# Spreading norm factors with one broadcast multiply and a float32 product, with sums and spreads called between contraction steps

## The chip, the cores and the metric

The kernel runs on one core of a Trainium2 chip. The metric is the device time of one execution in microseconds (us), lower being better; the runs of the kernel before took 1409.04 to 1411.53 us, with a median of 1411.13. Engines are named as in the profile: PE is TensorE's products, PEld its loads of the stationary operand, DVE is VectorE, ACT is ScalarE, POOL is GpSimd and SP issues most transfers.

## What is computed

A model of two layers over 512 tokens of width 1024, in float32. Layer 0 is a forgetting attention of 16 heads, layer 1 a latent attention (queries from 768, keys and values from 256 latent values, 16 heads, a rotary part of 64), and each layer ends in a gated feed-forward block with a convolution of width 3. What matters here is the norm, which stands in front of each block, twice more inside the latent attention and once at the end:

```python
def rmsnorm(x, g):
    y = x * lax.rsqrt(jnp.mean(x * x, axis=-1, keepdims=True) + EPS)
    return y * g

ckv = rmsnorm(x, kv_in_g) @ w_dkv
latent = rmsnorm(ckv[..., :KV_LORA], kv_norm_g)
k_rope = apply_rope(ckv[..., KV_LORA:], cos, sin)
q = rmsnorm(h @ w_dq, q_norm_g) @ w_uq
u = rmsnorm(x, ffn_norm) @ w_in
```

## The kernel before

Activations lie transposed: a tile has 128 features on the partitions and the 512 tokens as columns. Every weight and activation is split into a high and a low float32r part, and one contraction step (`mm3`, L82 to L85) is three products of 128x128 by 128x512: high by high, high by low, low by high. A projection tile is 8 such steps (6 or 2 from the latents) into one PSUM bank of the pool "acc", which has 3 banks; attention scores, transposes and the norms use the pool "att" with 5. `load_w` (L87) fetches a weight tile through SP, casts the high part on ScalarE (L104) and subtracts the low part on VectorE or GpSimd (L105).

A norm's factor belongs to a token, so it is needed along the columns, the same on all partitions. It is made in these steps. `Squares.add` (L137 to L145) squares a feature tile and adds it to a running sum. `rstd_of` (L147) contracts the sum with a vector of ones on TensorE, in four products of 128 tokens each (L153), so that the sums come out with tokens on the partitions, 128x4; VectorE scales them (L156) and GpSimd takes the power -0.5 (L158). `bcast_ps` (L161) spreads them back: it splits the factors into a float32r high part (the cast L165) and a low part (L166), scales the identity by each of the four columns of each part (eight operations of 128x128, L171) and contracts both 128x512 results with a matrix of ones (two float32r products, L172). `bcast` (L175) copies the result from PSUM on ScalarE (L179).

The norm is never applied to the input of a product but to its result. `Rstd.after` (L276) is called after each of the first tiles of a block: after the first complete tile it calls the sums, after the second the spread, and then it runs the evacuations that had to wait. `ffn` and `down` use it; `down` (L630) is a projection of the latent attention's preparation: six query tiles, then the rotary key tile, then two key/value tiles. Between these, in program order, stand the sums of the query norm (after the rotary key tile) and its spread (after the first key/value tile). `latents` (L637) multiplies a tile by the spread factors (L640) and splits it (L188 on ScalarE, L189 on VectorE). The first rotary product, `mm_rope(0)`, takes all six query latents. `turn` (L665) evacuates a rotary product: four copies of 32 partitions on ScalarE, which exchange halves (`swapped`, L647), then a multiply by the cosine on VectorE (L669). The key/value norm adds two squares (L145) and calls its sums after `mm_rope(0)`, its spread after the first query product, `proj_q(0)`.

The last norm of the program works on two halves of 256 tokens, with the second half's chain at the very end.

The program is written in the order above, and a planner puts the instructions of each engine into a fixed order: it takes what it expects to be ready, the earliest in the program first. Semaphores are placed by it too, and each engine then runs its list in order.

Of the kernel before, what the change touches and what calls it, by code (L numbers as in the profile page):

```python
# [15 lines left out]
P = 128  # L16
# [29 lines left out]
def tile_kernel(ctx, tc, xT_d, gains_d, bf_d, const_d, conv_d, wv_d, wq_d, wk_d, wfo_d,  # L46
# [77 lines left out]
    ones_r = cp.tile([P, P], F32R, name="ones_r")  # L124
    v.memset(f(ones_r), 1.0)
# [35 lines left out]
    def bcast_ps(r, m=NT):  # L161

        two = T(sp, [P, 2, NT], F32R, "two", 2)
        rh, rl = two[:, 0, :m], f(two[:, 1, :m])
        v.tensor_copy(rh, r)  # L165
        v.tensor_tensor(out=rl, in0=r, in1=f(rh), op=ALU.subtract)  # L166
        pt = att()[:, :m * P]
        for j, part in enumerate((f(rh), rl)):
            d = T(cp, [P, 512], F32R, "r2", R2)[:, :m * P]
            for i in range(m):  # L170
                v.tensor_scalar(out=d[:, i * P:(i + 1) * P], in0=idf, scalar1=part[:, i:i + 1], scalar2=None, op0=ALU.mult)  # L171
            pe.matmul(pt, ones_r, d, start=(j == 0), stop=(j == 1))  # L172
        return pt
# [95 lines left out]
    class Rstd:  # L269


        def __init__(self, squares):
            self.squares, self.step, self.R, self.todo = squares, 0, None, []

        def after(self, evacuate):
            if self.R is None:  # L276
                self.todo.append(evacuate)
                if self.step == 0:
                    self.r = rstd_of([self.squares.sum], D)
                else:  # L280
                    self.R = bcast(self.r)
                    for e in self.todo:
                        e(self.R)
                self.step += 1
            else:
                evacuate(self.R)


    def ffn(layer, xs, squares, gbase):
        with tc.tile_pool(name=f"ffn{layer}", bufs=1, reuse_waits="tile") as fp:  # L290
# [21 lines left out]
            for j in range(KF):  # L312
                for b in range(2):
                    wh, wl = load_w(wfi_d[layer, j, b], [P, KD, P])
                    pt = acc()
                    for k in range(KD):
                        mm3(pt, (wh[:, k, :], wl[:, k, :]), parts(xs, k), k == 0, k == KD - 1)
                    rstd.after(lambda R, j=j, b=b, pt=pt: evacuate(j, b, pt, R))
# [303 lines left out]
    with tc.tile_pool(name="ml", bufs=1, reuse_waits="tile") as mp:  # L622
# [7 lines left out]
        def down(w_d, gbase, dst):  # L630
            wh, wl = load_w(w_d, [P, KD, P], gain=(KD, gains[:, gbase:gbase + KD]))
            pt = acc()
            for k in range(KD):
                mm3(pt, (wh[:, k, :], wl[:, k, :]), parts(xs, k), k == 0, k == KD - 1)
            rstd.after(lambda R: v.tensor_tensor(out=dst, in0=pt, in1=R, op=ALU.mult))
# [29 lines left out]
        def turn(pt):  # L665

            c, t_ = r2(), r2()
            swapped(t_, pt, MSCALE)
            v.scalar_tensor_tensor(out=c, in0=pt, scalar=MSCALE, in1=cosT, op0=ALU.mult, op1=ALU.mult)  # L669

            def end():
                v.tensor_tensor(out=t_, in0=t_, in1=sinT, op=ALU.mult)
                v.tensor_tensor(out=c, in0=c, in1=t_, op=ALU.add)
                return c

            return end
# [55 lines left out]
        for j in range(KQ):  # L732
            down(wdq_d[j], G_MLA, qc[:, j, :])
            if j:
                for i in ((0, 1) if j == 1 else (j,)):
                    squares.add(qc[:, i, :], a, v if j == KQ - 1 else g)
# [3 lines left out]
        down(wdkv_d[KL], G_KVIN, krt)  # L740
        r = rstd_of([squares.sum], QL)
        down(wdkv_d[0], G_KVIN, qc[:, KQ, :])
        Rq = bcast(r, T(mp, [P, S], F32, "e3", 2))
# [8 lines left out]
        squares = Squares()  # L752
        for k in range(KL):
            squares.add(qc[:, KQ + k, :], a, v)
# [4 lines left out]
        r = rstd_of([squares.sum], KVL)  # L759
# [147 lines left out]
```

## Time and profile before

| what | value |
|---|---|
| median of 3 runs | 1411.13 us (1409.04 to 1411.53) |
| the profiled execution, its own time | 1410.6 us |
| its span, first to last instruction | 1408.8 us |
| TensorE busy | 1373.6 us, 98% of the span, 6594 products |
| VectorE, ScalarE, GpSimd busy | 886.6, 648.7 and 282.2 us |
| mean granted TensorE clock | 0.993 |

Busy time of TensorE is pipelined time: one entry's duration is longer than the distance to the next. Where a price is worked out, the distance between two starts is taken. An entry of a timeline shows in brackets how long its engine had been idle and what ended that. In a timeline, neighbouring entries of the same kind are merged, with their number behind the x.

### The profile page before, as it was taken

Reading aid. Unit: us, or ns where it says so; the run is one execution under the profiler, and the core shown is the slowest. Engines: PE = TensorE matmul, PEld = TensorE weight load, DVE = VectorE, ACT = ScalarE, POOL = GpSimd, SP = SyncE. Lnnn points to the kernel's source line nnn. Section 1 sums busy time; section 2 is a strip of 40 time slices with the busy share of each in tenths; the row PEclk is TensorE's granted clock in tenths of the full one; section 3 lists DMA queues with packets and bytes.
Section 4 is the critical chain, followed back from the end, with each engine's and each line's share of the span. In section 5 each row is a group of like instructions: output and inputs, shape, how many; then the busy total and the mean of one; then the engine's idle time right before and its main releaser. Section 6 shows DMA issues by size and latency. Waiting matters only on the chain. (4 is left out here: it accounts for less than half of the span.)

```text
span 1408.8 us, 17333 instructions
## 1 busy us (share of the span) xinstructions
PE 1373.6 (98%) x6594; PEld 1150.8 (82%) x6594; DVE 886.6 (63%) x1482; ACT 648.7 (46%) x1131; POOL 282.2 (20%) x214
## 2 busy tenths in 40 slices
PE   8999999899999999999899999999999999999997
PEld 7988888788888888888688888888888888888886
DVE  6667785677777754445866665575557777774333
ACT  4588884254444432223556555653234444442111
POOL 4343323500000001145422222212210000000222
PEclk9999999999999999999999999999999999999999
DMA  5321112232323233332121111212222322323331
GB/s 180 103 77 54 56 54 68 78 105 90 103 92 99 96 94 96 97 117 83 41 68 50 55 60 51 72 60 90 91 97 96 95 100 95 100 92 92 97 99 70
DMA packets 41252, 120.23 MB, mean 85 GB/s; under 512 B 5552, under 2 KB 9952, under 8 KB 41168
## 3 DMA queue, kind: packets, MB, share of 16 engines
q1 hardware_dynamic: 39184, 117.00, 26.0%
q0 software_dynamic: 1840, 2.09, 0.6%
q8 instruction: 51, 0.84, 0.2%
q14 instruction: 33, 0.27, 0.1%
q10 hardware_dynamic: 144, 0.03, 0.0%
HBM read 116.74 MB, written 2.36 MB: 85 GB/s over the span
## 5 line engine op out<-in xcount | busy, mean ns | idle before, releaser
L83 PE MATMUL acc<-big,whi 128*128 128x512 f32 (+1 forms) x1504 | 587.2, 391 | 2.7 <-ACT big L188 1.7
L85 PE MATMUL acc<-big,wlo 128*128 128x512 f32 (+1 forms) x1504 | 584.8, 389 | 3.5 <-DVE wlo L105 3.5
L84 PE MATMUL acc<-big,whi 128*128 128x512 f32 (+1 forms) x1504 | 584.8, 389 | 1.2 <-DVE big L189 1.2
L104 ACT CAST whi<-raw 128x1024 fp32r<-128x1024 f32 (+5 forms) x243 | 229.2, 944 | 413.8 <-PE acc L84 281.6
L85 PEld LDWEIGHTS acc<-big,wlo 128*128 128x128 f32 x1504 | 283.9, 189 | 63.4 <-DVE wlo L105 4.1
L83 PEld LDWEIGHTS acc<-big,whi 128*128 128x128 f32 x1504 | 283.6, 189 | 61.5 <-ACT big L188 3.1
L84 PEld LDWEIGHTS acc<-big,whi 128*128 128x128 f32 x1504 | 284.0, 189 | 59.1 <-DVE big L189 1.8
L105 DVE TENSOR_TENSOR wlo<-raw,whi 128x1024 fp32r<-128x1024 f32 (+3 forms) x179 | 234.6, 1310 | 141.7 <-ACT whi L104 139.1
L141 POOL TENSOR_TENSOR r<-xT 128x512 f32<-128x512 f32 x28 | 31.3, 1122 | 724.0 <-DVE xT L264 402.7
L105 POOL TENSOR_TENSOR wlo<-raw,whi 128x768 fp32r<-128x768 f32 (+3 forms) x64 | 108.0, 1687 | 251.1 <-ACT whi L104 205.5
L304 DVE SCALAR_TENSOR_TENSOR c<-u,conv,c 128x510 f32<-128x510 f32 (+1 forms) x176 | 131.2, 748 | 3.5 <-ACT c L302 0.6
L299 DVE TENSOR_TENSOR u<-acc,R 128x512 f32<-128x512 f32 x88 | 60.3, 688 | 76.3 <-PE acc L85 76.3
L214 ACT ACTIVATE e<-e,nm 128x128 f32<-128x128 f32 (+3 forms) x128 | 71.2, 557 | 41.7 <-DVE nm L208 41.7
L145 POOL TENSOR_TENSOR r<-r,r 128x512 f32<-128x512 f32 x38 | 72.1, 1898 | 28.2 <-ACT r L139 21.3
L302 ACT ACTIVATE c<-u,conv 128x512 f32<-128x512 f32 x88 | 71.3, 813 | 3.1 <-DVE u L299 2.7
L308 ACT ACTIVATE sg<-c 128x512 f32<-128x512 f32 x44 | 27.8, 632 | 78.9 <-DVE c L304 78.8
L241 DVE TENSOR_TENSOR ptl<-att,pth 128x512 fp32r<-128x512 f32 (+3 forms) x128 | 55.5, 483 | 5.9 <-ACT pth L240 5.3
L185 ACT CAST big<-sg 128x512 fp32r<-128x512 f32 x32 | 19.9, 621 | 81.7 <-DVE sg L309 81.6
L217 DVE TENSOR_SCALAR e<-e,rl 128x128 f32<-128x128 f32 (+3 forms) x128 | 55.7, 495 | 1.2
L240 ACT CAST pth<-att 128x512 fp32r<-128x512 f32 (+3 forms) x128 | 46.8, 434 | 6.1 <-PE att L237 5.5
L237 PE MATMUL att<-idf,e 128*128 128x128 f32 x320 | 43.5, 275 | 0.5
L237 PEld LDWEIGHTS att<-idf,e 128*128 128x128 f32 x320 | 36.9, 140 | 8.5 <-DVE nm L208 3.8
(183 smaller groups left out, 1473.3 us busy)
## 6 DMA issues: line engine op xcount, KB each, us to landing
raw<-in_wfi SPq DMA_DIRECT2D x88, 512.0 KB, 3.5
raw<-in_wfu SPq DMA_DIRECT2D x32, 512.0 KB, 3.5
raw<-in_wmo SPq DMA_DIRECT2D x16, 512.0 KB, 3.5
raw<-in_wfu SPq DMA_DIRECT2D x16, 384.0 KB, 3.1
raw<-in_wuqn SPq DMA_DIRECT2D x16, 384.0 KB, 2.9
raw<-in_wq SPq DMA_DIRECT2D x8, 512.0 KB, 3.5
raw<-in_wk SPq DMA_DIRECT2D x8, 512.0 KB, 3.5
raw<-in_wv SPq DMA_DIRECT2D x8, 384.0 KB, 2.9
```

The costliest lines, as they stand in the source:

```text
L83: pe.matmul(out, wh, xh, start=start, stop=False)
L84: pe.matmul(out, wh, xl, start=False, stop=False)
L85: pe.matmul(out, wl, xh, start=False, stop=stop)
L104: a.copy(hi[:, c], raw[:, c])
L105: (eng or v).tensor_tensor(out=lo[:, c], in0=raw[:, c], in1=f(hi[:, c]), op=ALU.subtract)
L145: (adder or g).tensor_tensor(out=self.sum, in0=self.sum, in1=sq, op=ALU.add)
L214: a.activation(es[i], es[i], AF.Exp, scale=-1.0, bias=nm[:, i:i + 1], accum_out=l[:, i:i + 1])
L217: v.tensor_scalar(out=es[i], in0=es[i], scalar1=rl[:, i:i + 1], scalar2=None, op0=ALU.mult)
L237: pe.transpose(out=pt[:, (i - j) * P:(i - j + 1) * P], in_=es[i][:, j * P:(j + 1) * P], identity=idf)
L299: v.tensor_tensor(out=u, in0=pt, in1=R, op=ALU.mult)
L302: a.activation(c, u, AF.Identity, scale=cw[:, 2:3], bias=cw[:, 3:4])
L304: v.scalar_tensor_tensor(out=c[:, s:], in0=u[:, :S - s], scalar=cw[:, 2 - s:3 - s], in1=c[:, s:], op0=ALU.mult, op1=ALU.add)
```

## The change

The spread uses one VectorE multiply, the identity repeated four times by the factors repeated 128 times, and one plain float32 product in place of the two float32r products; the split into two parts goes. `Rstd` counts contraction steps instead of tiles: the sums come after step 11, the spread after step 18 (third step of the second tile, second step of the third). In the latent attention the sums of the query norm are called after the third step of the rotary key tile and its spread after the first step of the first key/value tile; the first query squares are added one tile later. The key/value norm no longer adds its two squares: both tiles are contracted with ones, in eight products. In `turn` the cosine multiply is written ahead of the four copies.

```diff
 def bcast_ps(r, m=NT):
-        two = T(sp, [P, 2, NT], F32R, "two", 2)
-        rh, rl = two[:, 0, :m], f(two[:, 1, :m])
-        v.tensor_copy(rh, r)
-        v.tensor_tensor(out=rl, in0=r, in1=f(rh), op=ALU.subtract)
-        pt = att()[:, :m * P]
-        for j, part in enumerate((f(rh), rl)):
-            d = T(cp, [P, 512], F32R, "r2", R2)[:, :m * P]
-            for i in range(m):
-                v.tensor_scalar(out=d[:, i * P:(i + 1) * P], in0=idf, scalar1=part[:, i:i + 1], scalar2=None, op0=ALU.mult)
-            pe.matmul(pt, ones_r, d, start=(j == 0), stop=(j == 1))
+        d, pt = r2()[:, :m * P], att()[:, :m * P]
+        v.tensor_tensor(out=d.rearrange("p (i t) -> p i t", i=m), in0=idf.unsqueeze(1).to_broadcast([P, m, P]),
+                        in1=r.unsqueeze(2).to_broadcast([P, m, P]), op=ALU.mult)
+        pe.matmul(pt, onesP, d, start=True, stop=True)
         return pt
...
+        def step(self):
+            self.steps += 1
+            if self.steps == KD + 3:
+                self.r = rstd_of([self.squares.sum], D)
+            if self.steps == 2 * KD + 2:
+                self.R = bcast(self.r)
+                for e in self.todo:
+                    e(self.R)
...
                         mm3(pt, (wh[:, k, :], wl[:, k, :]), parts(xs, k), k == 0, k == KD - 1)
+                        rstd.step()
...
+                if k in between:
+                    between[k]()
...
             c, t_ = r2(), r2()
+            v.scalar_tensor_tensor(out=c, in0=pt, scalar=MSCALE, in1=cosT, op0=ALU.mult, op1=ALU.mult)
             swapped(t_, pt, MSCALE)
-            v.scalar_tensor_tensor(out=c, in0=pt, scalar=MSCALE, in1=cosT, op0=ALU.mult, op1=ALU.mult)
...
-            if j:
-                for i in ((0, 1) if j == 1 else (j,)):
+            if j > 1:
+                for i in ((0, 1, 2) if j == 2 else (j,)):
...
-        down(wdkv_d[KL], G_KVIN, krt)
-        r = rstd_of([squares.sum], QL)
-        down(wdkv_d[0], G_KVIN, qc[:, KQ, :])
-        Rq = bcast(r, T(mp, [P, S], F32, "e3", 2))
+        down(wdkv_d[KL], G_KVIN, krt, {2: q_sums})
+        down(wdkv_d[0], G_KVIN, qc[:, KQ, :], {0: q_factors})
+        Rq = norm["R"]
...
-        squares = Squares()
+        kv_sq = []
         for k in range(KL):
-            squares.add(qc[:, KQ + k, :], a, v)
+            kv_sq.append(r2())
+            a.activation(kv_sq[k], qc[:, KQ + k, :], AF.Square)
...
-        r = rstd_of([squares.sum], KVL)
+        r = rstd_of(kv_sq, KVL)
```

`q_sums` and `q_factors` are functions that call `rstd_of` and `bcast` for the query norm; `onesP` is the matrix of ones in float32.

## Rows read from the trace of the kernel before

**Rows 1.** The page: busy time, share of the span, instructions of TensorE.

```profile
PE 1373.6 (98%) x6594; PEld 1150.8 (82%) x6594; DVE 886.6 (63%) x1482; ACT 648.7 (46%) x1131; POOL 282.2 (20%) x214
```

**Rows 2.** Timeline of TensorE, 663 to 708: start us, duration us; waits in brackets.

```profile
674.19 0.47 PE L172 MATMUL att<-r,ones_r 128*128 128x512 f32 x1 [0.21 <-DVE r L171]
675.89 0.50 PE L172 MATMUL att<-r,ones_r 128*128 128x512 f32 x1 [1.23 <-DVE r L171]
...
686.16 0.50 PE L83 MATMUL acc<-big,whi 128*128 128x512 f32 x1 [0.40 <-ACT big L188]
687.63 1.05 PE L153 MATMUL att<-small,r 128*128 128x2 f32 x8 [0.97 <-DVE r L145]
...
701.87 0.50 PE L83 MATMUL acc<-big,whi 128*128 128x512 f32 x1 [1.25 <-ACT big L188]
703.25 0.80 PE L84 MATMUL acc<-big,whi 128*128 128x512 f32 x1 [0.88 <-DVE big L189]
```

**Rows 3.** Table by stage: stretch, length, busy of five engines, clock, DMA, GB/s.

```profile
684.00:692.80 8.80, 7.13 (x25) 5.13 (x26) 6.02 (x9) 3.61 (x6) 3.96 (x4) 0.81 0.16 47
...
701.80:707.30 5.50, 4.55 (x13) 3.44 (x14) 3.32 (x5) 2.39 (x6) 1.91 (x2) 0.69 0.22 72
```

**Rows 4.** Timeline of TensorE, first norm's spread.

```profile
35.24 0.47 PE L172 MATMUL att<-r,ones_r 128*128 128x512 f32 x1 [0.44 <-DVE zn L450]
...
36.26 0.41 PE L172 MATMUL att<-r,ones_r 128*128 128x512 f32 x1
```

**Rows 5.** Timeline of TensorE: the cumulative float32 products; the feed-forward spread.

```profile
43.20 2.33 PE L463 MATMUL att<-e,z 128*16 128x512 f32 x8
45.46 0.44 PE L426 MATMUL acc<-whi,big 128*128 128x384 f32 x1
...
278.70 0.62 PE L172 MATMUL att<-r,ones_r 128*128 128x512 f32 x2
279.15 0.39 PE L83 MATMUL acc<-big,whi 128*128 128x512 f32 x1
```

**Rows 6.** Timelines of VectorE and GpSimd; a tile's group (min/median/max ns).

```profile
274.90 1.65 DVE L171 TENSOR_SCALAR r<-idf,two 128x128 fp32r<-128x128 f32 x8
...
671.02 4.81 DVE L171 TENSOR_SCALAR r<-idf,two 128x128 fp32r<-128x128 f32 x8
...
671.23 1.29 POOL L746 TENSOR_TENSOR kn<-kn,cosT 128x512 f32<-128x512 f32 x1 [0.52 <-ACT kn L647]
...
L640 DVE TENSOR_TENSOR r<-big,e x7: 679/683/2336, 677.1 to 699.7; 128x512 f32<-128x512 f32 x7
```

**Rows 7.** Timeline of TensorE: the sums of the first feed-forward block.

```profile
272.31 0.95 PE L153 MATMUL att<-small,r 128*128 128x2 f32 x8
```

**Rows 8.** Timeline of VectorE: first evacuations of the first feed-forward block.

```profile
280.90 1.28 DVE L299 TENSOR_TENSOR u<-acc,R 128x512 f32<-128x512 f32 x2
```

**Rows 9.** Timeline of VectorE: the last square of the query norm added.

```profile
664.31 0.69 DVE L145 TENSOR_TENSOR r<-r,r 128x512 f32<-128x512 f32 x1
```

**Rows 10.** Timeline of VectorE: the key/value norm between power and spread.

```profile
690.27 0.16 DVE L166 TENSOR_TENSOR two<-rstd,two 128x4 f32<-128x4 f32 x1
695.11 0.69 DVE L669 SCALAR_TENSOR_TENSOR r<-acc,cosT 128x512 f32<-128x512 f32 x1 [4.68 <-ACT r L647]
```

**Rows 11.** Waits (total us, times, longest), then ScalarE's timeline in the steady state.

```profile
DVE r L669 <- ACT r L647: 42.9, 8, 5.5
PE acc L703 <- DVE Vp L707: 4.9, 7, 0.7
...
784.48 2.39 ACT L647 ACTIVATE r<-acc 32x512 f32<-32x512 f32 x4
787.84 0.40 ACT L214 ACTIVATE e<-e,nm 128x128 f32<-128x128 f32 x1 [0.96 <-DVE nm L208]
```

**Rows 12.** The chain that ended last, in order of time, at the end.

```profile
1400.18 0.18 DVE two L165
...
1401.08 0.70 PE att L172 x2
```

More of the change, by code (lines that the diff above doesn't have):

```diff
@@ L123, in tile_kernel @@
     v.memset(ones, 1.0)
-    ones_r = cp.tile([P, P], F32R, name="ones_r")
-    v.memset(f(ones_r), 1.0)
+    onesP = cp.tile([P, P], F32, name="onesP")
+    v.memset(onesP, 1.0)
     v.memset(mhalf, -0.5)
@@ L272, in __init__ @@
         def __init__(self, squares):
-            self.squares, self.step, self.R, self.todo = squares, 0, None, []
+            self.squares, self.steps, self.R, self.todo = squares, 0, None, []
+        def step(self):
[6 more added lines that the diff above has]
+                    e(self.R)
         def after(self, evacuate):
@@ L277, in after @@
                 self.todo.append(evacuate)
[L278 to L284, printed above, removed]
             else:
@@ L628, in tile_kernel, with down @@
         rstd = Rstd(squares)
-        def down(w_d, gbase, dst):
+        def down(w_d, gbase, dst, between=()):
             wh, wl = load_w(w_d, [P, KD, P], gain=(KD, gains[:, gbase:gbase + KD]))
             pt = acc()
+            between = dict(between)
             for k in range(KD):
                 mm3(pt, (wh[:, k, :], wl[:, k, :]), parts(xs, k), k == 0, k == KD - 1)
+                rstd.step()
+                if k in between:
+                    between[k]()
             rstd.after(lambda R: v.tensor_tensor(out=dst, in0=pt, in1=R, op=ALU.mult))
@@ L739, in tile_kernel, with q_sums, q_factors @@
         krt, krs = kr[:, 0, :], kr[:, 1, :]
-        down(wdkv_d[KL], G_KVIN, krt)
-        r = rstd_of([squares.sum], QL)
-        down(wdkv_d[0], G_KVIN, qc[:, KQ, :])
-        Rq = bcast(r, T(mp, [P, S], F32, "e3", 2))
+        norm = {}
+        def q_sums():
+            norm["q"] = rstd_of([squares.sum], QL)
+        def q_factors():
+            norm["R"] = bcast(norm["q"], T(mp, [P, S], F32, "e3", 2))
+        down(wdkv_d[KL], G_KVIN, krt, {2: q_sums})
+        down(wdkv_d[0], G_KVIN, qc[:, KQ, :], {0: q_factors})
+        Rq = norm["R"]
         latents(0, KQ - 2, Rq, G_Q)
```

## The prediction

> **What bounds the kernel now.** I read the page first: TensorE is busy nearly the whole span [rows 1], so the program is a stream of products, and a change counts in two ways only: it adds or removes work on TensorE, or it removes or makes a hole in that stream. Then I asked for TensorE's own timeline and kept the entries with a wait in front of them, from the stage in which the latent attention is prepared. The reader is to see six holes within 30 us [rows 2]: two in front of the products that spread the query norm's factors, two around the first rotary product and the sums of the key/value norm, two after that norm's factors were spread. The table by stage adds that TensorE was granted only 0.81 and 0.69 of its clock in two stretches there, a mixture of its levels 2.4 and 1.2 GHz, after it had stood idle [rows 3]. So holes are paid for twice. Outside this stage the spreads leave little: in the first feed-forward block the spread and the sums stand with no wait in front of them [rows 5, 7].
>
> One more thing is read before costing. The two spread products of the first norm stand at 35.24 and 36.26 [rows 4] with four value products of a later loop turn between them, though the program writes the two together. The order on an engine is therefore planned from priorities and expected readiness; a line of the program states a priority, not a place. A moved call lands near its new place only if its input is expected by then.
>
> **The float32 product.** It replaces two float32r products of 128x512. Before, a pair took 279.15-278.70 = 0.45 us of TensorE [rows 5]. The only plain float32 product with wide columns is the cumulative one: four products of 512, 384, 256 and 128 columns, 1280 together, issued as eight passes, from 43.20 to 45.46 [rows 5]: 2.26/1280 = 1.77 ns a column, 0.90 us for 512. So +0.45 us for each of six full spreads, +2.7 us in all if TensorE pays everywhere. Its stationary operand has 16 columns there against 128 here; the sums load 128x128 float32 tiles for eight passes within 0.95 us [rows 7], so the load hides. Ends: 0 (hidden in a hole) and 0.9 a spread; I take 0.45, the row of the same width.
>
> **The broadcast multiply.** Eight scalings took 1.65 us undisturbed and 4.81 us where GpSimd's multiplies for the rotary key ran beside them, the first at 671.23 [rows 6]; a cast and a subtraction stand ahead of them. One multiply of 128x512 takes its place: a two-input one takes 0.68 us, 2.34 at worst [rows 6]. No row has an operand that steps by nothing; I take 0.69 and keep 0.35 (half of it, an estimate) to 2.34. Eight small operations can meet a GpSimd instruction eight times, one large one once. The Trainium skill, "SBUF — State Buffer", section "Who interferes with whom", makes the pair of ports shared with GpSimd an exclusive lock, and its summary counts a VectorE operation with two SBUF inputs among those that wait in full. That speaks against the multiply being immune; by it one blocked multiply would end 1.65 us later (2.34-0.69) and the sum below would give back that much.
>
> **Feed-forward blocks and the first latent norm (three spreads).** The sums move three contraction steps later, the spread two. Cover: the first evacuations began at 280.90 [rows 8]; two steps (six products of 0.227 us) and the longer product move them by 1.8 us, the multiply's 0.96 us saving aside, to 282.7 and the first ends near 283.4. The fourth product needs that accumulator and would start after 24 products from 279.15, at 284.6, plus 0.45. Cover remains; without it the cost would be the excess, at most 1.8 us once per block. VectorE's queue behind it shifts by the same amount and has idle time. So only +0.45 each.
>
> **Query norm.** Removed: the waits 0.21+1.23 = 1.44 us [rows 2], made by the 4.81 us of scalings. The sums are now called after the third step of the key product that before ran ahead of them. The last square was added at 664.31 and done at 665.00 [rows 9]. The third step of that product ends near 664.0 (24 products of 0.227 us before the sums at 667.4), so TensorE could stand 1.0 us; the planned order may let later steps pass. Taken +0.5 (0 to 1.1). Queued behind are the rest of that product and all after it. The factors then come some 6 us earlier, and the latents with them.
>
> **First rotary product.** Holes 0.40+0.97 us [rows 2] and lost clock (1-0.81) x 8.8 = 1.67 us [rows 3]; the causes are late latents and the addition of two squares on VectorE that the change deletes. Of 3.04 us I take 0.8, -2.4. Instead the sums contract both squares on TensorE, twice the passes: at most +0.95 [rows 7], taken +0.9.
>
> **Key/value norm.** The power was done before the subtraction at 690.27, yet VectorE did nothing more until the rotary multiply L669 at 695.11, which waited 4.68 us for ScalarE's four copies [rows 10]; the scalings stood behind it. With that multiply written ahead of the copies and one multiply for eight scalings, the factors can be there before the next query product ends. Removed: 1.25+0.88 us [rows 2] and (1-0.69) x 5.5 = 1.71 us of clock [rows 3], together 3.84; 0.8 of it is -3.1.
>
> **The swap in the rotation, steady state.** In all eight places VectorE waited for the copies, 42.9 us in total, the copies being 2.39 us of each [rows 11]. TensorE feels it seven times as 0.70 us in front of a value product, behind VectorE's queue, 4.9 us in all [rows 11]. Now ScalarE waits for the multiply's 0.69 us; queued behind it are the exponentials, which before stood idle 0.96 us for VectorE [rows 11]. So they start some 0.96-0.69 = 0.3 us earlier, and I take 7 x 0.3 = -2.1 (ends 0 and -4.9). The multiply reads nothing that the copies write, so the rows alone leave open why it waited. The Trainium skill, "PSUM — Partial Sum Buffer", section "PSUM bank collisions raise a hardware error", has software order any two engines on one bank, reads included; by it the wait turns round instead of vanishing. The trace's 42.9 us agree.
>
> **First norm and tail.** The wait of 0.44 us [rows 4] goes: -0.4. At the end, from the cast at 1400.18 to the end of the two half products (1401.08+0.70 = 1401.78) pass 1.60 us [rows 12]. After: a 256-column multiply (0.35 to 0.42, an estimate from 0.69), 256 x 1.77 = 0.45 us of product, some 0.25 us of latency: 1.1. So -0.5 (0 to -1).
>
> **The sum.** +2.7 -1.44 +0.5 -2.4 +0.9 -3.1 -2.1 -0.4 -0.5 = -5.8 us. The profiled execution took 1410.6 us (span 1408.8), so 1404.8; it lay 0.5 us below the median 1411.13 of the runs. Forecast 1405.3 us.
>
> **The rivals.**
> The holes move on (0.17): the latents, not the factors, hold TensorE. For it: the holes at 701.87 and 703.25 name the splitting of latents [rows 2], and ScalarE and GpSimd have the same work. Then only the query spread's 1.44, half of the holes and clock behind (3.4 of 3.04+3.84 = 6.9) and the edges' 0.9 come back, against 2.7+0.5+0.9: -1.6 us, 1409.5 on the median.
> More is recovered (0.17): every hole of the preparation, its clock and the value waits go, no new one comes: +2.7+0.9-1.44-3.04-3.84-4.9-0.9 = -10.5, 1400.6. For it: the query factors gain 6 us on a need that they missed by 1.23 us.
> Slower (0.08): float32 passes without cover. If the holes before and after are refilled by the scheduled order and nothing is gained beyond the query spread's wait, the bill is 2.7+0.9+1.1 (the early sums) -1.44 = +3.3 us, 1414.4. It decides once less than 3.3 us of the 6.9 us of holes and clock and the 4.9 us of value waits are won. Against it: the scalings' 4.81 us stand in front of a product in the rows.
> The swap does nothing (inside the forecast): if the wait were for a buffer, not the bank, 2.1 us stay: 1407.4.
>
> **How the numbers follow.** The forecast's own case has 0.58 and spans 1401.5 to 1408.3. The range takes in the case of more and the case of moved holes, 1398.5 to 1410.5, leaving out the slower case and the extremes. A measurement of this kernel tells about 0.2% (2.8 us, so 1408.3) from no change. Faster: the forecast and the larger gain, nearly whole, and a little of the moved holes: 0.77. Same: 0.15. Slower: 0.08.
>
> **What would show it.** Right: one VectorE multiply per spread near 0.69 us; float32 spreads of two passes with 0.9 us to the next product; no wait at the query spread; granted clock near 1 in the stage after the first rotary product; L669's waits shorter by some 2 us each and the value waits below 0.7. Wrong: waits of 1 us in front of the query sums; holes of the old size in front of the key product of the latents; the multiply stretched to 2 us beside GpSimd; the copies, now second, delaying exponentials and score evictions.

## The result: 1403.09 us, and the profile after

The changed kernel took 1403.09 us, the median of 4 runs (1401.83 to 1404.44); the kernel before took 1411.03 us in the same series. The ratio is 0.9948, 95% interval 0.9933 to 0.9962, so it is faster, by about 0.5%. The forecast was 1405.3. The profiled execution took 1403.26 us with a span of 1401.2, against 1410.6 and 1408.8 before: 7.6 us of span to account for. A later series (e14 below) puts the same two kernels 5.9 us apart, so the size is known to some 2 us.

The page of the changed kernel, busy times:

```profile
PE 1369.7 (98%) x6602; PEld 1149.8 (82%) x6602; DVE 877.3 (63%) x1417; ACT 649.8 (46%) x1131; POOL 280.6 (20%) x214
```

TensorE is busy 3.9 us less than in [rows 1], and the span fell by more: holes are part of it. Where it came from is found by setting the same instruction of both traces side by side along the program. Four rows of the kernel before, from the timelines of ScalarE and TensorE (start us, duration us): the load of the Exp table that opens the preparation, the first latent score product, the last value products of the heads, the sums of the first half of the last norm.

```profile
663.68 1.28 ACT L737 ACT_TABLE_LOAD   x1
707.29 2.07 PE L203 MATMUL att<-kn,tn 128*128 128x128 f32 x12
962.10 0.81 PE L725 MATMUL acc<-ptl,Vp 128*128 128x512 f32 x4
1392.02 0.95 PE L153 MATMUL att<-small,r 128*128 128x2 f32 x8
```

The same four of the kernel after:

```profile
663.93 1.28 ACT L738 ACT_TABLE_LOAD   x1
701.85 2.38 PE L197 MATMUL att<-kn,tn 128*128 128x128 f32 x12
954.07 0.81 PE L726 MATMUL acc<-ptl,Vp 128*128 128x512 f32 x4
1384.44 0.95 PE L153 MATMUL att<-small,r 128*128 128x2 f32 x8
```

The reader is to see the differences: +0.25, -5.44, -8.03, -7.58. So everything up to the table load gave +0.25 us, **the preparation -5.69** (43.61 us became 37.92), **the heads -2.59**, the second feed-forward block +0.45, the end almost nothing. Both gains and the one visible loss lie in stages that the prediction named. The border between preparation and heads is not sharp: right behind it the kernel after gives 0.3 us back (its twelve score products take 2.38 us, those of the kernel before 2.07). The distance from table load to first score product is the yardstick for the preparation in all that follows. For the heads it is the period, the mean distance over six repetitions between the value products that wait, once in two heads: (920.42-728.12)/6 = 32.05 us before, (912.31-722.54)/6 = 31.63 after.

Now TensorE's timeline after, the waits of the preparation and the spreads, against [rows 2, 4, 5]:

```profile
34.39 1.10 PE L166 MATMUL att<-r,onesP 128*128 128x512 f32 x2 [0.43 <-DVE z L444]
...
280.02 1.02 PE L166 MATMUL att<-r,onesP 128*128 128x512 f32 x2
...
669.48 1.02 PE L166 MATMUL att<-r,onesP 128*128 128x512 f32 x2
669.94 0.80 PE L83 MATMUL acc<-big,whi 128*128 128x512 f32 x1
670.58 0.40 PE L84 MATMUL acc<-big,whi 128*128 128x512 f32 x1
...
682.92 0.50 PE L85 MATMUL acc<-big,wlo 128*128 128x512 f32 x1 [1.72 <-POOL wlo L105]
685.55 1.62 PE L153 MATMUL att<-small,r 128*128 128x2 f32 x14
692.91 1.10 PE L166 MATMUL att<-r,onesP 128*128 128x512 f32 x2 [0.16 <-DVE r L164]
698.75 0.50 PE L84 MATMUL acc<-big,whi 128*128 128x512 f32 x1 [0.43 <-DVE big L183]
699.89 0.50 PE L84 MATMUL acc<-big,whi 128*128 128x512 f32 x1 [0.18 <-DVE big L183]
```

The six holes of [rows 2], 4.94 us, were not quite all: the timeline before has two smaller waits between them, 0.28 us at 684.81 and 0.32 us at 697.81. Eight waits of 5.54 us in the preparation have become four of 2.49 us, and the largest is a new one, 1.72 us, in front of a third pass that wants a low weight part from GpSimd. The query spread at 669.48 has no wait. The float32 product and the product behind it hold TensorE until the next regular start: 670.58-669.48 = 1.10 us, less the 0.23 us of the product between, 0.87 us for the spread. The table by stage of the kernel after (columns as in [rows 3]):

```profile
684.00:692.80 8.80, 8.75 (x47) 7.19 (x45) 4.56 (x7) 4.29 (x8) 4.50 (x4) 1.00 0.25 75
692.80:701.80 9.00, 8.28 (x32) 5.96 (x33) 7.81 (x11) 5.67 (x11) 2.46 (x3) 1.00 0.28 86
```

The granted clock was 0.81 and 0.69 in the two stretches of [rows 3]; here it is 1.00, and 1.00 over the whole preparation from 663.93 to 701.85, where the kernel before had 0.92. No stretch of the preparation runs at the lower level any more, although 1.72 us of idle time stand in it.

In the heads, the list of waits of the kernel after (total us, times, longest), to set beside [rows 11]:

```profile
DVE r L669 <- PE acc L85: 20.8, 8, 2.9
...
PE acc L704 <- DVE Vp L708: 5.4, 7, 0.8
```

VectorE's 42.9 us of waits for ScalarE's copies are gone; the rotary multiply now waits for the product itself. The value products' wait did not shrink; it grew from 4.9 to 5.4 us, although the heads gained. How that goes together is read below, at the swap.

### The profile page after: what moved, and what is told of

Read it like the earlier page. It is cut to its first block, busy times and chain, and to the rows that moved or that the text cites. A ratio compares the mean times of both kernels' runs of the same rounds, so it can differ in the third digit from the quotient of the medians.

```text
span 1401.2 us, 17280 instructions
## 1 busy us (share of the span) xinstructions
PE 1369.7 (98%) x6602; PEld 1149.8 (82%) x6602; DVE 877.3 (63%) x1417; ACT 649.8 (46%) x1131; POOL 280.6 (20%) x214
## 4 chain that ended last, share of the span: by engine, by line
PE 88%; ACT 5%; DVE 4%; issue 1%; POOL 1%; DMA 1%; SPq 0%; DVEq 0%; POOLq 0%; ACTq 0%
PE acc L83 25%; PE acc L84 25%; PE acc L85 25%; PE att L197 4%; PE acc L726 2%; PE acc L565 1%; PE att L231 1%; ACT pth L234 1%; ACT r L648 1%; ACT e L208 1%; DVE big L183 1%; PE att L83 1%; PE att L85 1%; PE att L84 1%; DVE ptl L235 1%
## 5 line engine op out<-in xcount | busy, mean ns | idle before, releaser
L208 ACT ACTIVATE e<-e,nm 128x128 f32<-128x128 f32 (+3 forms) x128 | 71.3, 559 | 33.6 <-DVE nm L202 33.4
L234 ACT CAST pth<-att 128x512 fp32r<-128x512 f32 (+3 forms) x128 | 46.9, 434 | 6.1 <-PE att L231 5.5
L231 PE MATMUL att<-idf,e 128*128 128x128 f32 x320 | 40.3, 272 | 0.0
```

The costliest lines, as they stand in the source:

```text
L208: a.activation(es[i], es[i], AF.Exp, scale=-1.0, bias=nm[:, i:i + 1], accum_out=l[:, i:i + 1])
L231: pe.transpose(out=pt[:, (i - j) * P:(i - j + 1) * P], in_=es[i][:, j * P:(j + 1) * P], identity=idf)
L234: a.copy(hi, pt[:, :w])
```

## The experiments

None leaves anything out: each kernel computes the same function, by a different order or by differently placed work. Medians of the kernel before in the three series were 1410.43 (e1 to e3, e6), 1409.91 (e4, e5, e8, e10) and 1410.26 us (e11 to e14); each ratio is to its own. Preparation and period come from the one profiled execution of each kernel. In the preparation TensorE ran at the lower level for 6.8 us in the kernel before, e2 and e3, for 3.4 us in e4, e11 and e12, and not at all in the others.

| kernel | median us | ratio to before | preparation us | period us |
|---|---|---|---|---|
| before | 1411.03 | | 43.61 | 32.05 |
| after | 1403.09 | 0.9948 [0.9933, 0.9962] | 37.92 | 31.63 |
| e1_no_swap | 1405.06 | 0.9960 [0.9948, 0.9973] | 36.90 | 31.98 |
| e2_swap_only | 1405.60 | 0.9962 [0.9950, 0.9975] | 41.59 | 31.64 |
| e3_spread_only | 1411.63 | 1.0007 [0.9998, 1.0016] | 42.40 | 32.02 |
| e4_query_calls_back | 1404.22 | 0.9956 [0.9944, 0.9969] | 38.95 | 31.66 |
| e5_add_back | 1402.72 | 0.9944 [0.9932, 0.9957] | 36.72 | 31.68 |
| e6_pair | 1402.42 | 0.9940 [0.9928, 0.9953] | 37.45 | 31.62 |
| e8_calls_only | 1405.62 | 0.9962 [0.9949, 0.9976] | 37.61 | 31.96 |
| e10_pair_low_parts | 1399.27 | 0.9920 [0.9907, 0.9934] | 34.55 | 31.62 |
| e11_query_calls_only | 1407.07 | 0.9976 [0.9966, 0.9985] | 40.66 | 32.0 |
| e12_key_sums_only | 1408.82 | 0.9990 [0.9980, 1.0000] | 41.82 | 32.05 |
| e13_pair_low_add | 1399.92 | 0.9931 [0.9918, 0.9943] | 35.51 | 31.68 |
| e14_changed_again | 1404.38 | 0.9956 [0.9944, 0.9969] | 37.94 | 31.64 |

### The swap in the rotation

**e1**: the changed kernel with the old order in the rotation.

```
-            v.scalar_tensor_tensor(out=c, in0=pt, scalar=MSCALE, in1=cosT, ...)
             swapped(t_, pt, MSCALE)
+            v.scalar_tensor_tensor(out=c, in0=pt, scalar=MSCALE, in1=cosT, ...)
```

> The changed kernel with turn as it was: copies first, cosine multiply behind them. Theory (the swap lets VectorE evict scores earlier, so that TensorE's ten transposes per pair of heads no longer stand for a score bank): the 7 pairs of heads give back about 0.4 us each, the ten transposes take 1.5 us to the next product again instead of 1.0, and the key/value factors wait behind the rotary multiply again, 1 to 3 us more; together 4 to 6 us slower than the changed kernel, some 1407 to 1409. Rival (the swap only turns the wait round and is worth nothing; the gain is that of the spreads and the calls): within 1 us of the changed kernel, 1403.

**e2**: the same two lines exchanged in the kernel before, and nothing else.

> The kernel before with only the swap in turn. Theory: the pairs of heads are 0.4 us shorter each (7 x 0.4 = 2.8 us) and the eight scalings of the key/value norm start earlier; 3 to 5 us faster than before, 1406 to 1408. Rival (swap worth nothing by itself, or only beside the new spread): 1411.

The periods settle whether it is the swap: 31.98 and 32.05 without it, 31.64 and 31.63 with it. The swap is worth 0.35 to 0.41 us per two heads whatever else is changed, and the rival that it does nothing falls. e2 gained some 4.8 us, as the theory said: 2.0 in the preparation, the rest in the heads. e1 lost only about 2 against the changed kernel, not 4 to 6: its preparation was 1.0 us shorter than the changed kernel's, not longer. With the calls moved, the multiply in front of the copies has nothing left to free in the preparation; the last two waits of the kernel after, 0.43 and 0.18 us, are not in e1's. Why the swap should bring them stays open.

The place is seen in the steady state. First the kernel before, timelines of TensorE and VectorE (ScalarE's copies and exponentials are in [rows 11]):

```profile
784.03 2.07 PE L203 MATMUL att<-kn,tn 128*128 128x128 f32 x12
786.91 0.69 DVE L669 SCALAR_TENSOR_TENSOR r<-acc,cosT 128x512 f32<-128x512 f32 x1 [5.53 <-ACT r L647]
787.23 1.78 PE L237 MATMUL att<-idf,e 128*128 128x128 f32 x10
788.77 0.36 PE L703 MATMUL acc<-whi,big 128*128 128x256 f32 x1
792.14 0.38 PE L703 MATMUL acc<-whi,big 128*128 128x256 f32 x1 [0.70 <-DVE Vp L707]
```

The kernel after, timelines of the same engines and of ScalarE:

```profile
778.16 2.07 PE L197 MATMUL att<-kn,tn 128*128 128x128 f32 x12
778.36 0.69 DVE L669 SCALAR_TENSOR_TENSOR r<-acc,cosT 128x512 f32<-128x512 f32 x1 [2.85 <-PE acc L85]
779.08 2.40 ACT L648 ACTIVATE r<-acc 32x512 f32<-32x512 f32 x4 [0.50 <-DVE r L669]
781.35 1.25 PE L231 MATMUL att<-idf,e 128*128 128x128 f32 x10
781.51 0.40 ACT L208 ACTIVATE e<-e,nm 128x128 f32<-128x128 f32 x1
782.36 0.36 PE L704 MATMUL acc<-whi,big 128*128 128x256 f32 x1
783.74 1.68 DVE L235 TENSOR_TENSOR ptl<-att,pth 128x512 fp32r<-128x512 f32 x4 [0.88 <-ACT pth L234]
785.81 0.38 PE L704 MATMUL acc<-whi,big 128*128 128x256 f32 x1 [0.77 <-DVE Vp L708]
```

Before, VectorE stood behind the copies and came late to the score evictions; ten transposes, whose weight loads wait for the evictions, took 788.77-787.23 = 1.54 us to the next product. After, the evictions are done in time and the ten take 782.36-781.35 = 1.01 us. The waits of the weight loads (PEld) are the sign: before, those of L237 waited for VectorE's L208 14 times, 3.8 us in all, and no such line is in the changed kernel's list; in e1 it is back with the same numbers, as its list of waits shows:

```profile
PEld att L231 <- DVE nm L202: 3.8, 14, 0.3
```

These 0.53 us are not the gain by themselves. In both kernels the value product that comes next stands waiting (0.70 us at 792.14, 0.77 us at 785.81), so it starts when the chain through ScalarE and VectorE has made its operand; that TensorE arrives sooner only makes the wait longer. The chain is: ScalarE's copies, exponentials and casts (L240 before, L234 after), then VectorE's subtraction, which waits 0.88 us for the casts, and behind it in VectorE's queue the value operand. Before, ScalarE finished the copies and then stood idle 0.96 us for the evictions [rows 11]. After, it stands idle 0.50 us for the multiply, and the exponentials follow the copies without a gap. From the first score product to the first exponential passed 787.84-784.03 = 3.81 us, and now 781.51-778.16 = 3.35; from the same product to the value product 792.14-784.03 = 8.11, and now 785.81-778.16 = 7.65. Both differ by 0.46 us, which is 0.96 less 0.50, in all seven places; e1 has the old distances and e2 the new ones. So the value products start earlier because the exponentials do, and their wait grew because the transposes in front of them end earlier still.

### Spread or calls

**e3**: the kernel before with only the new spread (the changed body of `bcast_ps` and its float32 ones).

> The kernel before with only the new spread (one broadcast multiply, one float32 product), all calls and the swap as before. Theory: the query norm's two waits of 0.2 and 1.2 us go, each spread costs TensorE 0.45 us more (about 0.9 us to the next product), so that five full spreads take back what the query norm gives; within 2 us of before, 1409 to 1412. Rival (the spread itself is the gain): 1406 or less.

**e8**: the reverse, the changed kernel with the old spread and the old order in the rotation; only the places of the sums and spreads and the separate squares are new.

```
     def bcast_ps(r, m=NT):
-        d, pt = r2()[:, :m * P], att()[:, :m * P]
...
+        for j, part in enumerate((f(rh), rl)):
+            for i in range(m):
+                v.tensor_scalar(out=d[:, i * P:(i + 1) * P], in0=idf, ...)
+            pe.matmul(pt, ones_r, d, start=(j == 0), stop=(j == 1))
```

> The kernel before with only the new places of the calls and the uncombined key/value squares; the old spread with eight scalings and the old turn. Theory: the calls are worth most of what happens in the preparation, 3 to 5 us, and need neither the new spread nor the swap; no gain in the pairs of heads; 1406 to 1408. Rival (the calls need the short spread, since eight scalings still stand beside GpSimd): 1410 or more.

The spread alone gave 1411.63, no gain; it saves 1.2 us in the preparation, and set beside the kernel before, its two feed-forward blocks and the first latent norm lose 0.45, 0.45 and 0.47 us, which uses that up. The calls alone gave 1405.62, and their preparation, 37.61, is as short as the changed kernel's with all parts. The reason stands in VectorE's timeline of e8:

```profile
669.80 1.65 DVE L171 TENSOR_SCALAR r<-idf,two 128x128 fp32r<-128x128 f32 x8
```

The eight scalings of the query norm took 1.65 us here, not 4.81 [rows 6]: called earlier, they are through at 671.45, before GpSimd begins with the rotary key at 677.19. The early call removes what the broadcast multiply was to remove. That is why the parts don't add.

**e11** and **e12** each take one of the moved calls into the kernel before: e11 calls the query sums and spread between contraction steps, as the changed kernel does; e12 gives the key/value squares to the sums one by one. What e8 has beside these two, the later calls of the block norms and of the first query squares, has no run of its own.

```
e11: +        down(wdkv_d[KL], G_KVIN, krt, {2: q_sums})
     +        down(wdkv_d[0], G_KVIN, qc[:, KQ, :], {0: q_factors})
e12: -            squares.add(qc[:, KQ + k, :], a, v)
     +            kv_sq.append(r2())
     +            a.activation(kv_sq[k], qc[:, KQ + k, :], AF.Square)
```

> The kernel before with only the query norm's sums and spread called early; old spread, old turn, old block norms, added key/value squares. Theory (the early query call is most of what the calls gain, and the parts overlap, which is why undoing it alone cost the changed kernel 1 us): 3 to 5 us come back in the preparation, 1406 to 1408. Rival (the gain of the calls lies in the uncombined key/value squares): less than 1.5 us, 1409 and above.

> The kernel before with only the two key/value squares contracted separately. Theory (the addition's wait of 1 us in front of the sums goes, the latents are as late as before and four more products are paid): between 1 us faster and 1 us slower than before, 1410 to 1411. Rival (the addition holds VectorE and with it the clock): 3 us or more faster, 1407 or less.

e11 shortened the preparation by 2.95 us, e12 by 1.8. (The profiled execution of e11 was the slowest of its runs, 1411.12 us, with a wait of 1.92 us at the first latent norm's spread, and that of e12 the fastest; both differences lie ahead of the stage compared here.) By their medians they gained 3.2 and 1.4 us; the first fits its theory, the second lies between its theory and its rival, and its interval touches 1. Together they shorten the preparation by 4.75 us, and e8 with all moved calls by 6.0. In e12 the two waits at the query spread stand as in [rows 2], 0.21 and 1.24 us; they are not the key/value sums' to close.

**e4** and **e5** take one part back from the changed kernel: e4 the query calls to their old lines, e5 the addition of the two key/value squares on VectorE.

```
e4: -        down(wdkv_d[KL], G_KVIN, krt, {2: q_sums})
    -        down(wdkv_d[0], G_KVIN, qc[:, KQ, :], {0: q_factors})
    +        down(wdkv_d[KL], G_KVIN, krt)
    +        q_sums()
    +        down(wdkv_d[0], G_KVIN, qc[:, KQ, :])
    +        q_factors()
e5: -        r = rstd_of(kv_sq, KVL)
    +        r = rstd_of([squares.sum], KVL)
```

> The changed kernel with the query norm's sums after the whole rotary key tile and its spread after the whole first key/value tile, as before. Theory (the early call is what brings the query latents in time and keeps the clock up through the first rotary product): the waits in front of the first rotary product's later steps come back, with a stretch at half clock behind them; 2 to 4 us slower than the changed kernel, 1405 to 1407. Rival (the single multiply alone cures the query norm, its place is worth nothing): within 1 us of the changed kernel, 1403.

> The changed kernel with the two key/value squares added on VectorE again and four products for the sums in place of eight. Theory (with the latents early, the addition has time; TensorE saves the 0.8 us of four products): between 1 us faster and 1 us slower than the changed kernel, 1402 to 1404. Rival (the addition was what held the sums, about 1 us of wait and a stretch at half clock): 2 us or more slower, 1405 and above.

e4 lost 1.0 us in the preparation and 1.1 by the medians, between its theory and its rival. The theory's mechanism is there: waits of 0.80, 0.56 and 0.28 us stand in front of steps of the first rotary product, and 3.4 us run at the lower clock behind them. But the changed kernel's own 1.72 us hole is gone, so that most of the loss is made good. e5 came out as its theory said, even: 1402.72. The addition brings back a wait of 0.62 us in front of the sums, and its preparation is yet 1.2 us shorter: the second set of sums on TensorE is gone, and so are the last three waits of the kernel after, 0.77 us. So in the changed kernel the separate squares are the one part that is worth nothing or less, while in the kernel before they were a gain.

### The price of the float32 product

**e6**: the changed kernel, but the factors split into two float32r parts, each made by one broadcast multiply and spread by a float32r product.

```
+        for j, part in enumerate((f(rh), rl)):
+            v.tensor_tensor(out=d.rearrange(...), in0=idf.unsqueeze(1).to_broadcast([P, m, P]),
+                            in1=part.unsqueeze(2).to_broadcast([P, m, P]), op=ALU.mult)
+            pe.matmul(pt, ones_r, d, start=(j == 0), stop=(j == 1))
```

> The changed kernel with the factors split in two float32r parts again, each spread by one broadcast multiply and contracted by a float32r product: two multiplies of 0.69 us and the two small operations in place of one, two products of 0.22 us in place of 0.9. Theory (TensorE pays the float32 product in full at the four spreads that have cover, VectorE's extra us is hidden there): 0.4 us less at each of the four, up to 1 us more at the end where VectorE's chain is open; 0 to 2 us faster than the changed kernel, 1401 to 1403. Rival (the shorter VectorE chain is what pays): 2 us or more slower, 1405 and above.

1402.42 us: 0.7 below the changed kernel, inside the 0 to 2 expected and inside the spread of the runs. The trace is sharper than the median: the second feed-forward block, which moved by +0.45 us in the changed kernel, moves by nothing in e6.

### The new hole

The 1.72 us in front of the third pass were followed on GpSimd and VectorE, timelines of the kernel after:

```profile
673.24 1.71 POOL L754 TENSOR_TENSOR kn<-kn,cosT 128x512 f32<-128x512 f32 x1 [5.58 <-ACT kn L648]
680.60 4.51 POOL L105 TENSOR_TENSOR wlo<-raw,whi 128x768 fp32r<-128x768 f32 x2
681.72 3.94 DVE L641 TENSOR_TENSOR r<-big,e 128x512 f32<-128x512 f32 x2
689.21 1.83 POOL L105 TENSOR_TENSOR wlo<-raw,whi 128x768 fp32r<-128x768 f32 x1 [3.54 <-ACT whi L104]
691.01 1.03 POOL L158 TENSOR_TENSOR rstd<-rstd,small 128x4 f32<-128x4 f32 x1
692.07 0.69 DVE L164 TENSOR_TENSOR r<-idf,rstd 128x512 f32<-128x512 f32 x1 [2.85 <-POOL rstd L158]
```

GpSimd's two subtractions for the first rotary weights wait behind the rotary key and then take 4.51 us beside VectorE's latent multiplies, which take 3.94 us for two where the median of one was 0.68 [rows 6]. All four are through at 681.72+3.94 = 685.66, 5.06 us after the first began; one after the other, at 1.83 us (the subtraction at 689.21) and 0.68, they would need 5.02. Taking turns would give just that. A third subtraction stands in front of the power of the key/value norm, for which the factors' multiply waits 2.85 us.

**e10**: e6, with the low weight parts of the first rotary and the first query product made on VectorE.

```
-            return mm_lat(load_w(wuqr_d[j], [P, KQ, P], eng=g), 0, KQ)
+            return mm_lat(load_w(wuqr_d[j], [P, KQ, P], eng=g if j else v), 0, KQ)
-            pt = mm_lat(load_w(wuqn_d[h], [P, KQ, P], eng=g), 0, KQ)
+            pt = mm_lat(load_w(wuqn_d[h], [P, KQ, P], eng=g if h else v), 0, KQ)
```

> The kernel with two broadcast multiplies and two float32r products per spread (e6_pair), and the low weight parts of the first rotary product and of the first query product subtracted on VectorE instead of GpSimd. Theory (the changed kernel's one new hole, 1.7 us in front of the first rotary product's third pass, is GpSimd working through the rotary key beside VectorE; and the key/value norm's power stands behind such a subtraction): the hole goes and the factors come 1 to 2 us earlier; 1 to 2 us faster than e6_pair, 1400.5 to 1401.5. Rival (VectorE is as crowded there and the hole only changes its name): 1402 to 1403.

1399.27 us, 10.6 below the kernel before of its series; the best of the study. The preparation fell to 34.55 us. All waits that TensorE has left up to the score products, from its timeline:

```profile
690.09 0.50 PE L172 MATMUL att<-r,ones_r 128*128 128x512 f32 x1 [0.23 <-DVE r L170]
695.14 0.50 PE L84 MATMUL acc<-big,whi 128*128 128x512 f32 x1 [0.20 <-DVE big L189]
698.26 2.09 PE L203 MATMUL att<-kn,tn 128*128 128x128 f32 x11 [0.26 <-DVE kn L658]
```

0.69 us in all, against 5.54 before; the last stands just behind the first score product. The result lies below the 1400.5 to 1401.5 expected. The hole that the changed kernel has at 682.92 (1.72 us there, 1.16 in e6) was GpSimd's load, as said.

**e13** joins e10 and e5 (the addition back), **e14** is the changed kernel again on the same chip.

> The kernel with pairs and low parts on VectorE (e10_pair_low_parts) with the two key/value squares added on VectorE again. Theory (four products fewer, 0.8 us, and the addition now meets little GpSimd work): 0.5 us faster to even, 1398.5 to 1399.5. Rival (VectorE, with two more subtractions, is late with the addition and TensorE waits): 1 us or more slower, 1400.3 and above.

> The changed kernel as it is, beside the others on this chip. Theory: 1402 to 1404, and 3 us or more slower than e13_pair_low_add. Rival (the difference to the last version is one of chips): within 1 us of it.

e13 did not add the two gains: 1399.92, between its theory and its rival, and a preparation 1.0 us longer than e10's. Its waits are the rival's: 0.61 us in front of the sums for the addition, 0.9 at the key/value spread. e14 gave 1404.38 us, a little above the 1402 to 1404 expected, with the same preparation as the first time, 37.94; between e13 and e14, on one chip, lie 4.5 us, so the gain of e10 and e13 over the changed kernel is not the chip's.

## Why the prediction was right, and where it was not

**The bound.** Right: the products barely changed, and both gains are holes and clock. Rival "the holes move on" falls, but for one hole, the 1.72 us. "More is recovered" lies 2.5 us below the result, and e10 shows that it was to be had, by other means. "Slower" falls by the result; even the new spread alone, with none of the moved calls, took only 1411.63 us (e3).

**Float32 product, broadcast multiply.** Right. 0.87 us for the spread where 0.90 was estimated; the multiply, in the kernel after, over all spreads (min/median/max ns):

```profile
L164 DVE TENSOR_TENSOR r<-idf,rstd x8: 426/692/693, 30.7 to 1392.3; 128x512 f32<-128x512 f32 x6, 128x256 f32<-128x256 f32 x2
```

692 ns against 0.69, and none of the eight was drawn out: each starts when the power that it waits for has just ended on GpSimd, and none has a GpSimd instruction beside it (at the key/value norm the next subtraction began at 693.09). In e10, which makes two per spread, two such multiplies took 2.93 us from 687.11, and a subtraction of GpSimd ran beside them from 687.23; the first took 0.68 us, the second 2.32. So the multiply is not immune; it met nothing in the changed kernel. The Trainium skill, "SBUF — State Buffer", section "Who interferes with whom", has a VectorE operation with two SBUF inputs contend with a GpSimd instruction that reads SBUF; the 2.32 us in e10 agree with it, and no multiply of the changed kernel came to the test.

**Feed-forward blocks and first latent norm.** The cover held in both blocks, and the price was the +0.45 forecast (the second block moved from -8.03 to -7.58). The first latent norm cost nothing: before, its sums waited 0.39 us for GpSimd's addition, at 633.30, and three steps later they don't. A credit of 0.39 us was overlooked.

**The preparation.** The terms there (+0.45, -1.44, +0.5; -2.4, +0.9; +0.45, -3.1) make -4.64; the trace shows -5.69. Two products that stand at the same place in both programs, behind the query spread and ahead of the key/value spread, divide it (TensorE's timeline, the kernel before, then the kernel after):

```profile
676.69 0.39 PE L85 MATMUL acc<-big,wlo 128*128 128x512 f32 x1
695.07 0.39 PE L85 MATMUL acc<-big,wlo 128*128 128x512 f32 x1
```

```profile
675.60 0.39 PE L85 MATMUL acc<-big,wlo 128*128 128x512 f32 x1
692.37 0.39 PE L85 MATMUL acc<-big,wlo 128*128 128x512 f32 x1
```

The differences are -1.09 and -2.70, and they began at +0.25 and end at -5.44. So the query norm gave -1.34 where -0.49 was forecast, the first rotary product with the key/value sums -1.61 (forecast -1.5), the key/value norm -2.74 (forecast -2.65). The term that was mis-sized is the query norm's. The brackets' 1.44 us count only idle time after the modelled end of the product in front; from the start of the last product ahead of the two spread products (673.59) to the first behind them (676.23) passed 2.64 us, and with the float32 product 1.10 (669.25 to 670.58, less the 0.23 of a product between), -1.54 where +0.45-1.44 = -0.99 was forecast. And of the +0.5 for sums called too early +0.24 came: no wait of more than 0.15 us stands in front of them, but the way across them took 1.27 us instead of 1.03.

The forecast's mechanism was right in three points: no wait at the query spread, no stretch at the lower clock, a key/value spread that waits 0.16 us. For the third it asked more than was needed: the rotary multiply ahead of the copies, with "one multiply for eight scalings", was said to bring the factors early, but e8 has neither, waits 0.50 and 0.23 us at that spread, and its preparation of 37.61 us is as short as the changed kernel's. What the prediction missed was that its causes were alternatives: e11, e12, the short spread and the swap, alone, shorten the preparation by 2.95, 1.8, 1.2 and 2.0 us, and all together it is 5.69, not 7.95.

**The swap in the steady state.** The mechanism held, and its size was a little small: the exponentials start earlier, and the value products with them. ScalarE's idle time fell from 0.96 us to 0.50, not to 0.69, because the multiply starts while ScalarE still has a weight cast to finish (778.18 to 778.59 in the kernel after). So each of the seven places gains 0.46 us instead of 0.3; the period shows 0.42, seven of them 2.9, of which -2.59 lies between the two rows of the heads, against -2.1. What failed is the sign by which it was to be seen, "the value waits below 0.7": they are 0.77 us, since the transposes ahead of them end 0.53 us earlier. The Trainium skill, "PSUM — Partial Sum Buffer", section "PSUM bank collisions raise a hardware error", has software order two engines on one bank, reads included; by it the wait turns round, and it did, onto ScalarE, from up to 5.5 us to 0.5. That the bank is the reason is not shown: no run lets the two read different banks.

**First norm.** Failed: the wait of 0.44 us is still 0.43. In the kernel after the factors' multiply is long done, in VectorE's timeline:

```profile
30.69 0.69 DVE L164 TENSOR_TENSOR r<-idf,rstd 128x512 f32<-128x512 f32 x1 [1.15 <-POOL rstd L158]
```

It ended at 31.38, three us before the product at 34.39. The wait names the gate's operation L444, the last reader of a tile of the pool "att", into which the spread product writes; [rows 4] named the gate too (L450). So the product waits for the gate and not for its factors, most likely for the bank, which no run tests. A shorter spread can't help there, and the products behind it come 0.36 us later, for the longer product.

**Tail.** -0.5 was forecast; in the profiled execution the way from the start of the power to the copy took 1394.14-1391.60 = 2.54 us against 2.42 before. VectorE's part is shorter, as e3 shows, but the product was longer. The last spread in the timeline of the kernel after, and of e3:

```profile
1391.60 0.70 POOL L158 TENSOR_TENSOR rstd<-rstd,small 128x2 f32<-128x2 f32 x1 [1.90 <-DVE rstd L156]
1392.91 1.19 PE L166 MATMUL att<-r,onesP 128*128 128x256 f32 x2 [1.58 <-DVE r L164]
1394.14 0.37 ACT L363 COPY r<-att 128x256 f32<-128x256 f32 x1 [2.67 <-PE att L166]
```

```profile
1400.68 0.70 POOL L158 TENSOR_TENSOR rstd<-rstd,small 128x2 f32<-128x2 f32 x1 [1.90 <-DVE rstd L156]
1401.98 0.67 PE L166 MATMUL att<-r,onesP 128*128 128x256 f32 x2 [1.58 <-DVE r L164]
1402.69 0.37 ACT L360 COPY r<-att 128x256 f32<-128x256 f32 x1 [2.15 <-PE att L166]
```

With the same waits the product took 1.19 us in the one and 0.67 in the other; the granted clock around it was 0.50 and 1.00 in the tables by stage, the lower and the upper level. In e3 the way is 2.01 us, 0.41 shorter than before, near the forecast.

**The sum.** -5.8 forecast, -7.6 measured in span. The preparation gave 1.05 us more than forecast, the heads 0.5 more, the end 0.5 less. Ahead of the preparation +0.25 came instead of +0.95: the first latent norm gave 0.6 more than forecast, the first norm 0.3 less, and 0.7 us came from the clock between the first attention and the feed-forward block. From 236 to 270 us it was 0.95 here and 0.90 before; the stretch at the lower level lasted 3.4 us here and 6.8 before. It lasts one or the other in kernels that are alike up to there (3.4 in the kernel after, 6.8 in e1), so this part is luck and not the change's. In the later series, 1410.26 less e14's 1404.38, the change is worth 5.9 us, close to the forecast; the forecast's nearness to either number is within what the runs differ by.

## What to carry to other kernels

Where several edits shorten the same wait, price each of them alone and then all but one: alternatives don't add, and here the moved calls alone shortened the preparation as much as all parts together. Where two engines read one accumulator, try the short reader first, and judge the effect by the distance between starts: here the wait that was watched grew, while the product behind it came earlier. After the gain, read the stage again: the next hole (GpSimd's weight parts) was worth 2.9 us of the preparation (e6 to e10), over a third of what the change gave.

## What the runs showed of the hardware that was not expected

- A plain float32 product of 512 columns stands as two entries in the trace and held TensorE for 0.87 us, two float32r products of the same width for 0.45.
- VectorE and GpSimd stretched each other, both of them: in the stretch from 680.6 two latent multiplies took 3.94 us and two subtractions 4.51, where the multiply's median was 0.68 us and a single subtraction at 689.21 took 1.83; together they took 5.06 us, as long as one after the other.
- A VectorE multiply of 128x512 whose two operands each repeat elements took 692 ns, one with plain operands 683 (median in [rows 6]).
- The same last product of 256 columns took 0.67 or 1.19 us with the clock at 1.00 or 0.50, with the same waits in front of it; what decides the level there stays open.
